# Attention by pairs of heads on the two halves of the TensorE array: unpadded keys, probabilities normalized before the transposes, values as the stationary operand, output laid out by features

## The chip, the cores and the metric

One core of one Trainium2 chip. The metric is device time in microseconds of one execution of the whole program (two layers of a small diffusion model), median of the runs; a change under about 3.4 us (0.2%) can hardly be told from none.

## The reference, cut to what matters

Each of two layers mixes tokens with a windowed softmax attention beside an mLSTM, and then applies an FFN (layer 0) or a mixture of 8 experts (layer 1). Attention has 8 query heads on 2 key heads of 64 features. It is computed three times: for 256 context tokens against themselves (layer 0; K = 256 keys), and for 256 image tokens against their window and the context (layers 0 and 1; K = 512 keys). All of it is float32.

```python
def sink_attention(qg, kv_sets, sink_g):            # per head: one extra logit, the sink, without a value
    s = einsum('bqhgd,bkhd->bhgqk', qg, k); s = where(mask, s, -inf); m = max(sink, s.max(-1))
    p = exp(s - m); denom = exp(sink - m) + p.sum(-1)
    return einsum('bhgqk,bkhd->bhgqd', p, v) / denom
def merge_groups(att, h_ml, o_pre, g_att, g_ml, w_out):
    att_n = rmsnorm(att, g_att)                      # over the 512 features of a token
    ml = headwise_rmsnorm(h_ml) * g_ml * sigmoid(o_pre)
    return concatenate([att_n, ml], -1) @ w_out
```

## The kernel before

Activations are kept feature-major (`xT`, and their split into a high and a low float32r part, `aH` and `aL`). A weight block comes by one DMA of 1 MB into a `raw` tile, ACT and DVE split it into H and L (L123, L124), and a product is three float32r matmuls (`mm3`, recorded at L227). Plain float32 matmuls, as in attention, appear in the trace as two MATMUL rows each.

`Mix.attention` (L926 to L1012) walks over 16 items, (query block of 128 tokens, head). `score` multiplies the 128 queries of two heads by the head's keys; `KV` holds each key head twice, in the upper and in the lower 64 partitions, with zeros in the other half, so that a head's matmul contracts over 128 partitions of which 64 are zero. `top` (DVE) adds the mask, takes the maximum over the keys and clips it by the sink; `expo` (ACT) makes the probabilities `P` and their sum; `trans` (PE) transposes P by blocks of 128 keys; `evac` copies the transposes to `pT`, in turn by DVE and ACT; `pv` makes pT the stationary operand (128 columns) and streams the 64 columns of the values `VA`. After 8 heads `pvout` (L988 to L997) computes the denominators, divides, and sums squares. `attention_out` (L1020 to L1042) scales the token-major AO by the root mean square, transposes it in 8 blocks and splits it into `aH` and `aL`.

The generator yields between its steps; `weave` interleaves it in program order with its neighbours: layer 0's context attention with the projections, the image attention of both layers with the mLSTM (`ml`) and with filler matmuls (layer 0: modulation products on 32-column tiles of the array, `ps_f<-raw,csil`, and the output projection; layer 1: the projection of the output gates, `ps_f<-aH,H`). The engines then work through an order that a scheduler sets from that program when the kernel is built; each engine keeps it strictly. PSUM banks are shared: two for scores (`s`), two (`t`) for the transposes, the mLSTM's value products and its transposes, one for the attention output (`o`).

The lines that the change and the steps of the prediction touch: KV L691, L705, L831, L841; score, top, expo, trans, evac, pv, pvout L940 to L997; attention_out L1026 to L1041; the mLSTM's end in layer 1: its normalization L1167, its transposes and products L1174, aH L1177 and aL on POOL L1178; the attention part of aL L1040.

## Time and profile before

| | |
|---|---|
| time, median of 3 runs (lowest to highest) | 1695.44 us (1695.27 to 1697.46) |
| profiled execution: span from first to last instruction | 1694.2 us, 1.2 us below the median (a time of its own is not listed for it) |
| mean granted TensorE clock | 0.991 |
| busy, of the span | PE 98%, PEld 82%, DVE 79%, ACT 60%, POOL 6% |
| matmul rows | 9194 |

How to read it: a MATMUL row's duration is its latency, and rows overlap; what a matmul costs is the distance from its start to the next start. Busy time alone therefore says little; the timeline, the windows and the chain of waits say which engine sets the pace of a stretch. The context attention runs from 101 to 155 us, the image attention of layer 0 from 180 to 241 us, and that of layer 1 from 769 to 830 us.

### The profile page before, as it was taken

To read this page: it belongs to the slowest core of one execution; us is meant where nothing else is said; L and a number is where in the kernel's file an instruction comes from. 1 tells how busy PE (TensorE), PEld (TensorE's weight loads), DVE (VectorE), ACT (ScalarE), POOL (GpSimd) and SP (SyncE) were. 2 spreads that over 40 slices of the span, in tenths; PEclk is the share of its full clock that TensorE was granted. 3 is DMA by queue.
4 is the path that set the end of the run, shared out by engine and by line. 5 is a ranking of instruction groups with operands and counts; after the bars stand their busy time and mean duration, and the time that the engine had idled before them with its cause. 6 is when DMAs were issued, how large, how long until landed. Compare 5 with 4: busy or idle time off the path is not lost.

```text
span 1694.2 us, 24338 instructions
## 1 busy us (share of the span) xinstructions
PE 1653.5 (98%) x9194; PEld 1392.9 (82%) x9194; DVE 1344.4 (79%) x2100; ACT 1008.1 (60%) x1466; POOL 105.7 (6%) x152
## 2 busy tenths in 40 slices
PE   8999999999999999999999999999999999999996
PEld 6779789988888889897898888888888888888885
DVE  3484678887667735788768898999999899998987
ACT  5533555642223224635548777877787777877775
POOL 2310111100000000201110000000000000000001
PEclk8999999999999999999999999999999999999998
DMA  9322544565548814441086999999999999999990
GB/s 309 116 66 75 169 155 140 160 223 182 170 166 278 297 63 138 142 139 51 26 326 230 359 356 353 336 354 364 352 353 321 368 361 357 341 333 358 357 340 27
DMA packets 222637, 407.08 MB, mean 240 GB/s; under 512 B 9776, under 2 KB 106288, under 8 KB 222512
## 3 DMA queue, kind: packets, MB, share of 16 engines
q1 hardware_dynamic: 220464, 404.38, 68.9%
q8 instruction: 74, 1.21, 0.3%
q10 hardware_dynamic: 2048, 1.07, 0.2%
q14 instruction: 51, 0.42, 0.1%
HBM read 404.38 MB, written 1.05 MB: 239 GB/s over the span
## 4 chain that ended last, share of the span: by engine, by line
PE 88%; DVE 7%; issue 2%; ACT 2%; DMA 1%; POOL 1%; ACTq 0%; DVEq 0%; POOLq 0%
PE ps_mm L227 57%; PE ps_s L227 17%; PE ps_t L227 4%; PE ps_t L231 3%; PE ps_f L227 3%; PE ps_o L227 2%; DVE L L124 2%; PE ps_sb L227 1%; DVE ca L776 1%; ACT H L123 1%; DMA tok<-in_x 0%; PE ps_mb L227 0%; DVE xn L539 0%; DMA raw<-in_w_mod 0%; POOL aL L551 0%
## 5 line engine op out<-in xcount | busy, mean ns | idle before, releaser
L123 ACT ACTIVATE H<-raw 128x1024 fp32r<-128x1024 f32 (+1 forms) x676 | 702.6, 1050 | 394.4 <-PE ps_mm L227 295.0
L124 DVE TENSOR_TENSOR L<-raw,H 128x1024 fp32r<-128x1024 f32 (+1 forms) x671 | 802.8, 1221 | 140.0 <-ACT H L123 134.4
L227 PE MATMUL ps_mm<-H,X 128*128 128x512 f32 (+1 forms) x1536 | 461.2, 379 | 0.0
L227 PEld LDWEIGHTS ps_mm<-H,X 128*128 128x128 f32 x1536 | 280.8, 188 | 55.9
L227 PE MATMUL ps_mm<-L,X 128*128 128x512 f32 (+1 forms) x768 | 288.6, 376 | 0.0
L227 PE MATMUL ps_mm<-aL,H 128*128 128x512 f32 (+1 forms) x752 | 257.8, 343 | 5.0 <-POOL aL L551 2.3
L227 PE MATMUL ps_mm<-aH,H 128*128 128x512 f32 (+1 forms) x752 | 259.5, 347 | 2.4 <-ACT aH L542 2.3
L227 PE MATMUL ps_mm<-aH,L 128*128 128x512 f32 (+1 forms) x752 | 256.4, 342 | 0.0
L227 PEld LDWEIGHTS ps_mm<-L,X 128*128 128x128 f32 x768 | 144.9, 189 | 27.5
L227 PEld LDWEIGHTS ps_mm<-aL,H 128*128 128x128 f32 x752 | 143.1, 190 | 22.8 <-POOL aL L551 3.1
L227 PEld LDWEIGHTS ps_mm<-aH,H 128*128 128x128 f32 x752 | 142.6, 191 | 21.6 <-ACT aH L542 2.5
L227 PEld LDWEIGHTS ps_mm<-aH,L 128*128 128x128 f32 x752 | 142.7, 190 | 16.6 <-DVE L L124 0.4
L227 PE MATMUL ps_s<-H,hH 128*128 128x512 f32 x352 | 140.5, 399 | 0.0
L227 PE MATMUL ps_s<-L,hH 128*128 128x512 f32 x352 | 139.1, 395 | 0.0
L227 PE MATMUL ps_s<-H,hL 128*128 128x512 f32 x352 | 138.8, 394 | 0.0
L611 DVE SCALAR_TENSOR_TENSOR macc<-raw,csil,macc 128x1024 f32<-128x1024 f32 x70 | 87.6, 1282 | 4.2 <-DMA raw<-in_w_mod 3.7
L227 PEld LDWEIGHTS ps_s<-H,hL 128*128 128x128 f32 x352 | 66.1, 188 | 15.9
L227 PEld LDWEIGHTS ps_s<-H,hH 128*128 128x128 f32 x352 | 66.2, 188 | 14.1
L227 PEld LDWEIGHTS ps_s<-L,hH 128*128 128x128 f32 x352 | 66.2, 188 | 13.8
L227 PE MATMUL ps_mm<-fH,H 128*128 128x512 f32 (+1 forms) x224 | 77.3, 346 | 0.0
L227 PE MATMUL ps_mm<-fL,H 128*128 128x512 f32 (+1 forms) x224 | 77.2, 345 | 0.0
L227 PE MATMUL ps_mm<-fH,L 128*128 128x512 f32 (+1 forms) x224 | 77.0, 344 | 0.0
(351 smaller groups left out, 2132.8 us busy)
## 6 DMA issues: line engine op xcount, KB each, us to landing
raw<-in_exp_w SPq DMA_DIRECT2D x264, 1024.0 KB, 5.9
raw<-in_w_mod SPq DMA_DIRECT2D x48, 1024.0 KB, 5.4
raw<-in_ffn_w SPq DMA_DIRECT2D x34, 1024.0 KB, 5.4
raw<-in_w_in SPq DMA_DIRECT2D x18, 1024.0 KB, 5.7
raw<-in_w_out SPq DMA_DIRECT2D x12, 1024.0 KB, 5.3
raw<-in_ffn_w SPq DMA_DIRECT2D x8, 768.0 KB, 4.5
tok<-in_ctx SPq DMA_DIRECT2D x2, 512.0 KB, 4.7
tok<-in_x SPq DMA_DIRECT2D x2, 512.0 KB, 7.0
```

What stands on the lines that cost most here:

```text
L123: nc.scalar.activation(h, src, AF.Copy)
L124: eng.tensor_tensor(l, src, h.bitcast(F32), op=OP.subtract)
L227: return self.eng.matmul(o, a, b, **kw)
L231: return self.eng.transpose(o, a, i)
L611: V.scalar_tensor_tensor(a, raw[:, q], c, a, op0=OP.mult, op1=OP.add)
L776: V.scalar_tensor_tensor(a, u[:, j:j + T], vc[:, w + 4 * j + chunk:w + 4 * j + chunk + 1], a, op0=OP.mult, op1=OP.add)
```

## The change

Items are now (query block, pair of heads): 8 per call instead of 16.

- KV loses its zero halves: key head kv stands in both halves of the partitions. The two scores of a pair contract over 64 partitions each, one on the upper and one on the lower 64 rows of the array, into two PSUM banks.
- The sink's exponential is taken per head (ACT, 128x1), the denominator is formed at once (`norm`), and ACT scales P in SBUF by its reciprocal before the transposes.
- The product with the values has VA as the stationary operand (64 columns, one half of the array's columns for each head) and streams the 128 columns of pT. The output comes with features on the partitions: O[64 features of a head, tokens].
- pvout is one ACT copy. attention_out squares and sums over features by ACT and DVE, reduces over the partitions with matmuls (`rstd_rows`), and multiplies by gain and norm on DVE; the 8 transposes and the ACT scaling go. Half of the low parts aL goes to POOL.
- A step of the generator yields four times instead of twice; the pools of P and pT have 4 buffers instead of 3.

```diff
-            self.KV = m.tile([128, 2, 2, 2 * T], F32, name="KV")
+            self.KV = m.tile([128, 2, 2 * T], F32, name="KV")
...
-            G.memset(self.KV, 0.0)
...
-            items = [(qb, h) for qb in range(2) for h in range(8)]
+            items = [(qb, c) for qb in range(2) for c in range(4)]
...
             def score(i):
-                PE.matmul(Sc[i][:, :K], Q[:, h // 2, qb * 128:(qb + 1) * 128], KV[:, h // 4, h % 2, :K],
-                          start=True, stop=True)
+                Sc[i] = [bank("s"), bank("s")]
+                for hf, r in halves:
+                    PE.matmul(Sc[i][hf][:, :K], Q[r, c, qb * 128:(qb + 1) * 128], KV[r, c // 2, :K],
+                              start=True, stop=True)
...
+                for hf, _ in halves:
+                    h = 2 * c + hf
+                    act(st[:, 2, qb, h:h + 1], sinkb[:, l, h:h + 1], AF.Exp, bias=st[:, 0, qb, h:h + 1])
+
+            def norm(i):
+                a, b, d = (st[:, k, qb, 2 * c:2 * c + 2] for k in (1, 2, 3))
+                V.tensor_tensor(d, a, b, op=OP.add)
+                V.reciprocal(d, d)
+                for hf, _ in halves:
+                    e = P[i][hf]
+                    act(e[:, :K], e[:, :K], AF.Copy, scale=d[:, hf:hf + 1])
...
             def pv(i):
                 for kb in range(nk):
-                    PE.matmul(O[qb][:, h * 64:h * 64 + 64], pt[:, kb * 128:(kb + 1) * 128],
-                              VA[:, kb, h // 4 * 64:h // 4 * 64 + 64], start=kb == 0, stop=kb == nk - 1)
+                    for hf, r in halves:
+                        PE.matmul(O[qb][r, c * 128:(c + 1) * 128], VA[:, kb, c // 2 * 64:c // 2 * 64 + 64],
+                                  pt[hf][:, kb * 128:(kb + 1) * 128], start=kb == 0, stop=kb == nk - 1,
+                                  skip_group_check=True)
...
+                act(AO[:, :, qb * 128:(qb + 1) * 128], O.pop(qb).rearrange("p (c q) -> p c q", c=4), AF.Copy)
...
-            for t in range(n + 5):
+            for t in range(n + 4):
                 at(expo, t - 1)
                 at(score, t)
-                at(trans, t - 3)
-                at(pv, t - 4)
+                at(pv, t - 3)
                 yield
-                at(evac, t - 3)
-                at(pvout, t - 4)
+                at(norm, t - 1)
                 at(top, t)
+                at(pvout, t - 3)
+                yield
+                at(trans, t - 1)
+                yield
+                at(evac, t - 1)
                 yield
...
         def attention_out(self, s):
-            for qb in range(2):
-                act(AO[:, qb], AO[:, qb], AF.Copy, scale=r[:, qb:qb + 1])
+            for j in range(4):
+                if j == 0:
+                    act(acc, AO[:, j], AF.Square)
+                else:
+                    q = tmp("sqa")
+                    act(q, AO[:, j], AF.Square)
+                    V.tensor_tensor(acc, acc, q, op=OP.add)
+            r = rstd_rows(acc, 512)
...
+            for j in range(4):
+                f = tmp("af")
+                V.scalar_tensor_tensor(f, AO[:, j], col("g_att", l * 4 + j), r, op0=OP.mult, op1=OP.mult)
+                H = aH[:, j, SL[s]]
+                act(H, f, AF.Copy)
+                (V, G)[j % 2].tensor_tensor(aL[:, j, SL[s]], f, H.bitcast(F32), op=OP.subtract)
```

How the order moves, at three places. The first is PE in the image attention of layer 1, in its second half, before (ps_s: scores; kc,P: transposes of probabilities; VA and pT: product with the values; VM and PTm: the mLSTM's product; ps_f: filler):

```order
L227 MATMUL ps_s<-KV,Q_x 128x512
L231 MATMUL ps_t<-kc,P 128x128 x4
L227 MATMUL ps_o<-VA,pT 128x64 x4
L227 MATMUL ps_t<-VM_c,PTm 128x129 x2
L227 MATMUL ps_t<-VM_x,PTm 128x129 x2
L227 MATMUL ps_t<-VM_c,PTm 128x129 x2
L227 MATMUL ps_t<-VM_x,PTm 128x129
L227 MATMUL ps_s<-KV,Q_x 128x512
L231 MATMUL ps_t<-kc,P 128x128 x4
L227 MATMUL ps_o<-VA,pT 128x64 x4
```

and of the change:

```order
L227 MATMUL ps_s<-KV,Q_x 128x512 x2
L231 MATMUL ps_t<-kc,P 128x128 x4
L227 MATMUL ps_o<-pT,VA 64x128 x8
L227 MATMUL ps_f<-aH,H_7379 128x256
L227 MATMUL ps_f<-aL_91,H_7379 128x256
L227 MATMUL ps_f<-aH,L_7380 128x256
L231 MATMUL ps_t<-kc,P 128x128 x4
L227 MATMUL ps_f<-aH,H_7419 128x256
L227 MATMUL ps_f<-aL_89,H_7419 128x256
```

A head's score, transposes and product became a pair's, and work on the whole array stands between two blocks on halves of it.

The second place is PE in the image attention of layer 0, near its middle, in the change (csil: modulation products on quarters of the columns):

```order
L227 MATMUL ps_o<-pT,VA 64x128 x8
L227 MATMUL ps_f<-raw_2071,csil 32x256
L227 MATMUL ps_t<-VM_c,PTm 128x129 x3
L227 MATMUL ps_s<-KV,Q_x 128x512
L231 MATMUL ps_t<-kc,P 128x128 x4
L227 MATMUL ps_s<-KV,Q_x 128x512
L227 MATMUL ps_f<-raw_2071,csil 32x256 x2
L227 MATMUL ps_t<-VM_c,PTm 128x129 x3
L227 MATMUL ps_f<-raw_2071,csil 32x256 x5
L231 MATMUL ps_t<-kc,P 128x128 x4
```

Before, a csil block stood whole (x8) and a score alone; now the two halves of this pair stand apart, with transposes between them, and the 8 csil matmuls of a block stand in three pieces (1, 2 and 5).

The third place is DVE at the end of layer 1's mixing (HM: the mLSTM's output, scaled by its norm; aL_89, aL_90 and af: attention's part of the output projection's operand; mf: the mLSTM's part), before:

```order
L124 TENSOR_TENSOR L_8146<-raw_7213,H_8145 128x1024
L513 SCALAR_TENSOR_TENSOR nb<-nb,nv 128x8
L1040 SCALAR_TENSOR_TENSOR aL_89<-ps_t,vc,aH 128x256
L515 SCALAR_TENSOR_TENSOR ny<-nb,nc 128x8
L1167 TENSOR_SCALAR HM<-HM,ny 128x128
L1040 SCALAR_TENSOR_TENSOR aL_90<-ps_t,vc,aH 128x256
L1040 SCALAR_TENSOR_TENSOR aL_89<-ps_t,vc,aH 128x256
L1167 TENSOR_SCALAR HM<-HM,ny 128x128
L1040 SCALAR_TENSOR_TENSOR aL_90<-ps_t,vc,aH 128x256
L1167 TENSOR_SCALAR HM<-HM,ny 128x128 x6
L1174 SCALAR_TENSOR_TENSOR mf<-ps_t,vc,SG_x 128x256 x3
```

and of the change:

```order
L515 SCALAR_TENSOR_TENSOR ny<-nb,nc 128x2
L515 SCALAR_TENSOR_TENSOR ny<-nb,nc 128x8
L1185 TENSOR_SCALAR HM<-HM,ny 128x128 x3
L1055 SCALAR_TENSOR_TENSOR af<-AO,vc,ps_t 128x256 x4
L1058 TENSOR_TENSOR aL_89<-af,aH 128x256
L1185 TENSOR_SCALAR HM<-HM,ny 128x128
L1058 TENSOR_TENSOR aL_90<-af,aH 128x256
L1185 TENSOR_SCALAR HM<-HM,ny 128x128 x4
L1192 SCALAR_TENSOR_TENSOR mf<-ps_t,vc,SG_x 128x256 x2
```

Four af products and two differences stand between the pieces of HM where four differences stood, and the two norms' root steps, of 128x2 and 128x8, now run side by side just ahead of it.

## Rows read from the trace of the kernel before

**Rows 1.** The page: busy time of each engine (share of the span, instructions), and the chain that ended last, by engine.

```profile
PE 1653.5 (98%) x9194; PEld 1392.9 (82%) x9194; DVE 1344.4 (79%) x2100; ACT 1008.1 (60%) x1466; POOL 105.7 (6%) x152
PE 88%; DVE 7%; issue 2%; ACT 2%; DMA 1%; POOL 1%; ACTq 0%; DVEq 0%; POOLq 0%
```

**Rows 2.** Busy time by windows: length, then busy us (instructions) of PE, PEld, DVE, ACT, POOL, granted clock, DMA share, GB/s. The first three hold the three attention calls; then the FFN, and the experts.

```profile
100.00:179.00 79.00, 77.95 (x490) 68.86 (x493) 44.98 (x120) 30.57 (x85) 8.34 (x16) 0.98 0.17 54
179.00:300.00 121.00, 118.95 (x965) 100.40 (x957) 100.46 (x341) 66.99 (x172) 17.00 (x40) 1.00 0.51 166
768.00:846.00 78.00, 76.32 (x523) 64.56 (x521) 61.55 (x201) 42.69 (x114) 14.31 (x26) 0.98 0.13 41
300.00:700.00 400.00, 396.81 (x2173) 340.44 (x2172) 276.24 (x390) 139.10 (x204) 16.71 (x20) 1.00 0.57 186
900.00:1600.00 700.00, 699.86 (x3316) 575.82 (x3315) 642.55 (x655) 552.46 (x619) 0.00 (x0) 1.00 0.98 348
```

**Rows 3.** Timeline of PE in the image attention of layer 0: start, us from the first start to the last end, then the operation, rows x count, array rows*columns in use, moving operand.

```profile
180.96 0.28 PE L227 MATMUL ps_mb<-MRH_c,one 128*128 128x256 f32 x1
181.07 0.28 PE L227 MATMUL ps_mb<-MRL_c,one 128*128 128x256 f32 x1
181.28 1.07 PE L227 MATMUL ps_f<-raw,csil 128*32 128x256 f32 x16
182.28 1.13 PE L227 MATMUL ps_s<-KV,Q_x 128*128 128x512 f32 x2
183.24 0.83 PE L227 MATMUL ps_t<-VM_c,PTm 128*128 128x129 f32 x6
183.91 1.03 PE L227 MATMUL ps_sb<-QM_c,KM_c 128*128 128x256 f32 x4
...
190.02 0.60 PE L231 MATMUL ps_t<-kc,P 128*128 128x128 f32 x4
190.46 1.03 PE L227 MATMUL ps_sb<-QM_c,KM_c 128*128 128x256 f32 x4
191.33 1.02 PE L227 MATMUL ps_s<-KV,Q_x 128*128 128x512 f32 x2
192.18 0.83 PE L227 MATMUL ps_t<-VM_c,PTm 128*128 128x129 f32 x6
192.85 0.60 PE L231 MATMUL ps_t<-kc,P 128*128 128x128 f32 x4
193.29 1.00 PE L227 MATMUL ps_o<-VA,pT 128*128 128x64 f32 x8
194.13 0.39 PE L231 MATMUL ps_f<-kc,modrow 128*128 128x128 f32 x2
```

**Rows 4.** The same view in the context attention of layer 0: matmuls that use 36 rows of the array, and one head's score.

```profile
148.91 0.56 PE L227 MATMUL ps_o<-VA,pT 128*128 128x64 f32 x4
149.40 0.25 PE L231 MATMUL ps_f<-kc,Fc 36*128 36x36 f32 x1
149.49 0.23 PE L231 MATMUL ps_f<-kc,g 36*128 36x36 f32 x1
149.55 0.23 PE L231 MATMUL ps_f<-kc,Fc 36*128 36x36 f32 x1
149.70 0.50 PE L227 MATMUL ps_mm<-aH,H 128*128 128x512 f32 x1
...
155.06 0.59 PE L227 MATMUL ps_s<-KV,Q_c 128*128 128x256 f32 x2
155.49 0.38 PE L231 MATMUL ps_t<-kc,P 128*128 128x128 f32 x2
```

**Rows 5.** The same view behind layer 0's mixing: a sum over partitions as `rstd_rows` makes it, and the float32r matmul behind it.

```profile
290.97 0.61 PE L227 MATMUL ps_f<-ones,sqacc 128*128 128x1 f32 x4 [0.47 <-DVE sqacc L491]
291.44 0.36 PE L227 MATMUL ps_mm<-aH,H 128*128 128x256 f32 x1
291.64 0.28 PE L227 MATMUL ps_mm<-aL,H 128*128 128x256 f32 x1
291.76 0.28 PE L227 MATMUL ps_mm<-aH,L 128*128 128x256 f32 x1
```

**Rows 6.** By tile, the vector work of attention: count, then the shortest, median and longest in ns, first and last start, forms.

```profile
L950 DVE TENSOR_TENSOR ps_s<-ps_s,kc x32: 280/299/300, 181.6 to 817.6; 128x128 f32<-128x128 f32 x32
L952 DVE TENSOR_REDUCE ast<-ps_s x48: 412/680/692, 103.0 to 817.9; 128x1 f32<-128x512 f32 x32, 128x1 f32<-128x256 f32 x16
L953 DVE TENSOR_TENSOR ast<-ast,nsink x48: 140/152/516, 103.4 to 819.1; 128x1 f32<-128x1 f32 x48
L958 ACT ACTIVATE P<-ps_s,ast x48: 456/680/722, 104.0 to 820.1; 128x512 f32<-128x512 f32 x32, 128x256 f32<-128x256 f32 x16
L958 ACT ACTIVATION_READ_ACCUMULATOR P<-ps_s,ast x48: 188/193/243, 104.4 to 820.7; 128x1 f32 x48
L989 ACT ACTIVATE ast<-ast x6: 195/208/248, 132.7 to 822.0; 128x8 f32<-128x8 f32 x6
L991 DVE RECIPROCAL ast<-ast x6: 191/194/203, 134.3 to 822.9; 128x8 f32<-128x8 f32 x6
L1026 ACT ACTIVATE AO<-AO,ny x6: 707/710/725, 171.9 to 834.3; 128x512 f32<-128x512 f32 x6
```

**Rows 7.** Timelines at the end of layer 1's mixing (engine in the third column): the mLSTM's norm and its operand on DVE, POOL's low part, and the two idle times of PE in the output projection (in brackets, with what ended them).

```profile
836.15 0.17 DVE L520 TENSOR_SCALAR nv<-ss 128x8 f32<-128x8 f32 x1 [0.47 <-ACT junk L1136]
839.08 0.47 DVE L1040 SCALAR_TENSOR_TENSOR aL<-ps_t,vc,aH 128x256 fp32r<-128x256 f32 x1
842.67 0.87 DVE L1174 SCALAR_TENSOR_TENSOR mf<-ps_t,vc,SG_x 128x256 f32<-128x256 f32 x2
843.67 3.79 POOL L1178 TENSOR_TENSOR aL<-mf,aH 128x256 fp32r<-128x256 f32 x4 [1.00 <-ACT aH L1177]
...
844.46 0.39 PE L227 MATMUL ps_mm<-aL,H 128*128 128x256 f32 x1 [0.25 <-POOL aL L1178]
846.12 0.39 PE L227 MATMUL ps_mm<-aL,H 128*128 128x256 f32 x1 [1.04 <-POOL aL L1178]
```

More of the change, by code (lines that the diff above doesn't have):

```diff
@@ L930, in attention @@
             wm, KV, VA, Q = self.wm, self.KV, self.VA, self.Q[s]
[L931 removed]
+            AO = wm.tile([128, 4, T], F32, tag="AO", name="AO", bufs=1)
             st = wm.tile([128, 4, 2, 8], F32, tag="ast", name="ast", bufs=2)
[L933 to L935 removed]
+            self.AO[s] = AO
+            items = [(qb, c) for qb in range(2) for c in range(4)]
@@ L936, in attention @@
             n = len(items)
             Sc, P, TB, PT, O = {}, {}, {}, {}, {}
+            halves = [(hf, slice(hf * 64, hf * 64 + 64)) for hf in range(2)]
             def score(i):
-                qb, h = items[i]
-                Sc[i] = bank("s")
-                PE.matmul(Sc[i][:, :K], Q[:, h // 2, qb * 128:(qb + 1) * 128], KV[:, h // 4, h % 2, :K],
-                          start=True, stop=True)
-            def top(i):
-                qb, h = items[i]
-                p = Sc[i]
-                if s == "x":
-                    kb, m = ((3, m01), (2, m10))[qb]
-                    V.tensor_tensor(p[:, kb * 128:(kb + 1) * 128], p[:, kb * 128:(kb + 1) * 128], m, op=OP.add)
-                m = st[:, 0, qb, h:h + 1]
-                V.tensor_reduce(m, p[:, :K], axis=AX.X, op=OP.max, negate=True)
-                V.tensor_tensor(m, m, nsink[:, l, h:h + 1], op=OP.min)
@@ L955, in expo @@
-            def expo(i):
-                qb, h = items[i]
-                e = P[i] = wm.tile([128, 512], F32, tag="P", name="P", bufs=3)
-                act(e[:, :K], Sc.pop(i)[:, :K], AF.Exp, bias=st[:, 0, qb, h:h + 1],
-                    accum_out=st[:, 1, qb, h:h + 1])
-            def trans(i):
-                t = TB[i] = bank("t")
-                e = P.pop(i)
-                for kb in range(nk):
-                    PE.transpose(t[:, kb * 128:(kb + 1) * 128], e[:, kb * 128:(kb + 1) * 128], ident)
@@ new lines, in top @@
+            def top(i):
+                qb, c = items[i]
+                for hf, _ in halves:
+                    p = Sc[i][hf]
+                    if s == "x":
+                        kb, m = ((3, m01), (2, m10))[qb]
+                        V.tensor_tensor(p[:, kb * 128:(kb + 1) * 128], p[:, kb * 128:(kb + 1) * 128], m, op=OP.add)
+                    h = 2 * c + hf
+                    V.tensor_reduce(st[:, 0, qb, h:h + 1], p[:, :K], axis=AX.X, op=OP.max, negate=True)
+                m = st[:, 0, qb, 2 * c:2 * c + 2]
+                V.tensor_tensor(m, m, nsink[:, l, 2 * c:2 * c + 2], op=OP.min)
@@ new lines, in expo @@
+            def expo(i):
+                qb, c = items[i]
+                P[i] = []
+                for hf, _ in halves:
+                    h = 2 * c + hf
+                    e = wm.tile([128, 512], F32, tag="P", name="P", bufs=4)
+                    P[i].append(e)
+                    act(e[:, :K], Sc[i][hf][:, :K], AF.Exp, bias=st[:, 0, qb, h:h + 1],
+                        accum_out=st[:, 1, qb, h:h + 1])
+                Sc.pop(i)
+                for hf, _ in halves:
+                    h = 2 * c + hf
+                    act(st[:, 2, qb, h:h + 1], sinkb[:, l, h:h + 1], AF.Exp, bias=st[:, 0, qb, h:h + 1])
@@ new lines, in norm @@
+            def norm(i):
+                qb, c = items[i]
+                a, b, d = (st[:, k, qb, 2 * c:2 * c + 2] for k in (1, 2, 3))
+                V.tensor_tensor(d, a, b, op=OP.add)
+                V.reciprocal(d, d)
+                for hf, _ in halves:
+                    e = P[i][hf]
+                    act(e[:, :K], e[:, :K], AF.Copy, scale=d[:, hf:hf + 1])
+            def trans(i):
+                TB[i] = []
+                for e in P.pop(i):
+                    t = bank("t")
+                    TB[i].append(t)
+                    for kb in range(nk):
+                        PE.transpose(t[:, kb * 128:(kb + 1) * 128], e[:, kb * 128:(kb + 1) * 128], ident)
@@ L975, in pv @@
+            def evac(i):
+                PT[i] = []
+                for hf, src in enumerate(TB.pop(i)):
+                    pt = wm.tile([128, 512], F32, tag="pT", name="pT", bufs=4)
+                    PT[i].append(pt)
+                    if hf:
+                        act(pt[:, :K], src[:, :K], AF.Copy)
+                    else:
+                        V.tensor_copy(pt[:, :K], src[:, :K])
             def pv(i):
-                qb, h = items[i]
+                qb, c = items[i]
                 pt = PT.pop(i)
-                if h == 0:
+                if c == 0:
@@ L984, in pvout @@
             def pvout(i):
-                qb, h = items[i]
-                if h < 7:
+                qb, c = items[i]
+                if c < 3:
                     return
-                V.tensor_tensor(st[:, 2, qb], st[:, 0, qb], sinkb[:, l], op=OP.add)
-                act(st[:, 2, qb], st[:, 2, qb], AF.Exp)
-                V.tensor_tensor(st[:, 3, qb], st[:, 1, qb], st[:, 2, qb], op=OP.add)
-                V.reciprocal(st[:, 3, qb], st[:, 3, qb])
-                V.tensor_tensor(AO[:, qb].rearrange("p (h d) -> p h d", h=8),
-                                O.pop(qb).rearrange("p (h d) -> p h d", h=8),
-                                st[:, 3, qb].rearrange("p (h a) -> p h a", a=1).to_broadcast([128, 8, 64]),
-                                op=OP.mult)
```

40 lines of the change are left out of this document (9 added, 31 removed).

## The prediction

> **What bounds the kernel now.** I read the page first, then the windows of the three attention calls, then PE's timeline in them, then the vector engines' rows, last the end of layer 1's mixing. PE is busy for 98% of the span and makes 88% of the chain that ended last [rows 1]. In the windows that hold attention it is busy for 77.95 of 79, 118.95 of 121 and 76.32 of 78 us; ACT stands at 39%, 55% and 55% there, DVE at 57%, 83% and 79%. In the FFN and the experts PE is busy throughout [rows 2]; the change leaves the order there as it is, so a microsecond that PE wins or loses in attention moves the end by one. DMA is at 0.13 to 0.51 in attention. So the change is priced in PE starts, and then it is asked where PE would have to wait.
>
> **What PE's rows cost.** The distance of starts counts. A head's score is two rows: 191.33 to 192.18, 0.86 us (K = 512); 0.43 us for K = 256 [rows 3, 4]. Its product with the values is 8 rows from 193.29 to 194.13, 0.84 us, or 0.21 per matmul of two rows [rows 3]; these stream only 64 columns each, so loading 128 weight columns is what they cost. Four transposes take 0.44 us (190.02 to 190.46), as they will afterwards.
>
> **Part 1: halves side by side.** That tiles of the array work at once is seen here for quarters of the columns: 16 csil rows of 256 columns take 1.00 us [rows 3], while 16 such rows one by one would take 3.4 us (0.215 each, by the two of the 256-key score [rows 4]). Halves of the columns with different moving data are the same case; halves of the rows are not shown by any row. I take both as fully side by side when the two stand together. The new order has 24 pairs of scores; 19 stand together, 5 are parted (3 in layer 0's image call, 1 in each other). Saved: 12 image pairs x 0.86 + 7 context pairs x 0.43 = 13.3 us. The value product keeps 160 matmuls, 0.21 each, 33.6 us in all; they now stream 128 columns. The nearest rows, 6 mLSTM products of 129 columns in 0.67 us [rows 3], make a matmul of two 0.224. In the new order they need 88 slots of one or two (80 would do if none were parted): 19.7 us. Saved: 13.9. Together 27.2 us.
>
> The Trainium skill weighs against full overlap: "TensorE: Matmul & The Clock Gate", Part 3, gives measured speedups of 3.07 for four row tiles and 2.38 for three column tiles. By these (0.77 and 0.79 of the ideal), as an estimate, the paired scores and products would take 8 us more than in my sum. The csil rows reach 3.4 of 4 with the cost of leaving included, 3.8 without, so the sum goes by the rows.
>
> **Part 2: changing the tiling.** Going to and from a part of the array costs PE time. Into csil: 181.07 to 181.28, 0.21 against the 0.11 of the step before. Out of it: 1.00 instead of 4 x 0.215 = 0.86, and the score behind it takes 0.96 instead of 0.86, since nothing hides its weight load [rows 3]. The 36-row matmuls show the same for rows: 0.49 instead of 0.42 going in, 0.15 instead of 0.06 coming out [rows 4]. So an entry costs 0.10 for emptying the array, and up to 0.10 more for an unhidden load of 128 columns. I take 0.20 for an entry into the row halves (128 columns), 0.15 for the column halves (64), 0.18 back to the whole array, 0.12 into csil. Counted in the new order beyond those of the old: 29 into row halves, 35 into column halves, 51 back, 7 more into csil: 5.8 + 5.2 + 9.2 + 0.8 = 21.1 us. Bounds: 0.10 each makes 12 us, 0.20 each 24. The higher end is nearer, because a score behind csil shows both parts each time.
>
> **Part 3: what the new order cuts up.** In layer 0's image call the csil blocks of 8 matmuls no longer stand whole; pieces of 1 to 8 need 30 groups of up to four where 24 did. 6 x 0.43 (a group is two rows deep, 0.215 each) = 2.6 us.
>
> **Part 4: attention_out.** 24 transposes go: 24 x 0.11 = 2.6 us. Three calls of rstd_rows come: 4 rows of one column, 0.47 us [rows 5], and 4 rows of 128 columns, 4 x 0.11 [rows 3], so 2.8 us. Net +0.2. The KV memset lies on POOL, busy 8.34 of 79 us [rows 2]; at no cost, and its cover stays.
>
> PE's own sum: -27.2 + 21.1 + 2.6 + 0.2 = **-3.3 us**. By call: context -0.7, layer 0 image +1.7, layer 1 image -4.4, and 0.2 for part 4.
>
> **Part 5: what PE may have to wait for.** ACT gets, per image call, 16 scalings of 512 columns in SBUF (nearest row L1026, 0.71) and 16 sink exponentials (L989, 0.21), 14.7 us, and loses about 2 us (two L1026, two L989, partly replaced by squares) [rows 6]. In layer 1 that takes ACT from 42.69 to some 55 of 78 us [rows 2], 71%; no bound by itself. DVE gains 8 sums and reciprocals (0.35 together) and loses 8 of the 16 minima (0.15) [rows 6]: +1.6 us. The chain from a pair's scores to its first transpose: two masks and maxima (2 x 0.98), a minimum 0.15, two exponentials with their sums read out (2 x 0.8), two sinks 0.42, a scaling 0.71: 4.8 us, plus what stands between on DVE and ACT. The scaling waits on ACT for DVE's reciprocal, and behind it queue the mLSTM's exponentials and the copies of pT. By the new order, at the prices above, PE has 5.7 to 7.5 us of other work between these two points in layer 1, and over 8 in layer 0. I allow 1.5 us of waits, all in layer 1 (nothing to 8).
>
> The end of layer 1's mixing is a chain off PE: the mLSTM's last product, its norm on DVE from 836.15, mf from 842.67, POOL's low parts to 847.46, and PE idles 0.25 and 1.04 us for them [rows 7]. Two things change there. Of the filler, 42 matmuls stood behind the mLSTM's last product and 33 do now, so 9 x 0.12 = 1.1 us moves ahead of it while the chain behind stays. And DVE has, between the norm and mf, six attention operations where it had four (0.47 each), three sums of squares ahead, and the two root chains side by side: about 2.0 us more. So 3.1 us of layer 1's 4.4 are given back there.
>
> **Sum.** -3.3 + 1.5 + 3.1 = +1.3 us on the profiled span of 1694.2; the median of the runs stands 1.2 above that span, so **1696.8 us**, which is no change that can be told (0.2%, 3.4 us).
>
> **Rivals.**
> - *Cheaper switches.* If the emptying alone counts (0.10), because PE often waits at those points anyway or the loads hide, part 2 is 12 us: 9 us better, 1687.8; with no waits in part 5's middle, 1686. For it: the first transposes behind a block load data that is ready. Against: every csil row shows the exposed load.
> - *The row halves overlap poorly.* PE takes the two float32 rows of one score before it starts the other half, or the halves share a path. No row shows row tiles at work together. With no overlap 13.3 us are lost: 1710; with the partial overlap of the skill's figures above, about 1705. This ends slower; it decides when a pair of scores of 512 keys takes over 1.1 us from its first start to the next block.
> - *The vector engines set layer 1's pace.* If the scaling waits behind mLSTM work on ACT in most of the 16 image pairs, at 0.5 us each beyond my 1.5: some 6 us more, 1703. For it: 83% and 79% on DVE and a chain through three strictly ordered engines. Against: the order gives 5.7 us or more of cover. The Trainium skill speaks for it: "TensorEngine Tiling (Array Packing)", PSUM Bottleneck, says that tiling speeds TensorE and not the emptying of PSUM, which then may bound.
>
> **How the numbers follow.** My forecast 0.44, cheaper switches 0.25, poor row overlap 0.13, vector engines 0.18. The forecast's own range is 1692 to 1701, most of it within 0.2%. Faster by over 0.2%: the second case and a little of the first, 0.27. Slower: the last two and the upper end of the first, 0.34. The same: 0.39. The range reaches from the cheap switches to the row halves without overlap, 1686 to 1709.
>
> **What would show it.** Right: a score pair's four rows in about 0.86 us, starting in twos a few ns apart; eight value products in some 0.9 us; 0.10 us more at each change of tiling and a longer first row behind it; PE idle at the end of layer 1 grown to 3 us or more while its chain through DVE and POOL stands. Wrong: scores that start one after another (second rival), first rows behind a block that are not longer (first), or idle PE before the transposes of P in layer 1 that add up to over 4 us (third). If PE's idle time in the three windows falls and the switches cost as said, my end of layer 1 is wrong.

## The result, and the profile after

The changed kernel takes **1709.1 us** (median of 6 runs, 1706.5 to 1710.4) beside 1696.4 us for the kernel before on the same chip: a ratio of 1.0067, 95% interval 1.0049 to 1.0085. It is slower, by over three times what can be told from no change; the forecast was no change, 1696.8. The profiled execution took 1708.6 us (span 1706.9, granted clock 0.986; before 1694.2 and 0.991). PE is busy 5 us longer in a span that is 12.7 us longer; ACT gained 31 us [rows 1]:

```profile
PE 1658.6 (97%) x9194; PEld 1373.5 (80%) x9194; DVE 1344.7 (79%) x2115; ACT 1039.0 (61%) x1556; POOL 107.6 (6%) x156
PE 86%; DVE 7%; ACT 2%; issue 2%; POOL 1%; DMA 1%; ACTq 0%; POOLq 0%; DVEq 0%
```

The windows that answer to [rows 2], in the same columns. In the third, layer 1's attention, PE is idle for 7.9 of 78 us where it was 1.7; but 3.4 of these are a wait ahead of layer 1 (for Fc, 3.42 us in both kernels) that ended just ahead of this window before, at 767.83, and lies inside it now. The clock of the first and third fell from 0.98 to 0.96; FFN and experts stand as before.

```profile
100.00:179.00 79.00, 77.31 (x472) 61.79 (x473) 41.71 (x107) 38.08 (x113) 7.49 (x12) 0.96 0.17 54
179.00:300.00 121.00, 118.60 (x947) 89.11 (x946) 98.97 (x351) 76.34 (x200) 21.87 (x46) 1.00 0.48 157
768.00:846.00 78.00, 70.10 (x489) 52.24 (x488) 57.39 (x174) 52.55 (x139) 11.70 (x25) 0.96 0.09 29
300.00:700.00 400.00, 396.51 (x2168) 339.99 (x2168) 276.94 (x375) 142.47 (x210) 15.43 (x18) 1.00 0.57 184
900.00:1600.00 700.00, 699.86 (x3317) 575.64 (x3317) 639.87 (x658) 553.19 (x623) 0.00 (x0) 1.00 0.96 343
```

Cut at the same PE rows, the two profiles differ by stretch as follows (us; the forecast's parts beside):

| stretch | before | after | difference | forecast |
|---|---|---|---|---|
| start, to the qt product behind PE's long wait | 99.6 | 100.4 | +0.8 | 0 |
| context call, to the first csil row | 78.8 | 80.0 | +1.2 | -0.7 |
| layer 0's image call and FFN, to layer 1's Fc transposes | 590.8 | 594.1 | +3.3 | +1.7 |
| layer 1, to the mLSTM's last product | 64.9 | 66.3 | +1.4 | -4.4 + 1.5 + 1.1 |
| from there to the router's first product | 17.3 | 22.9 | +5.6 | 3.1 - 1.1 |
| the rest, to PE's last row | 829.0 | 829.4 | +0.4 | 0 |

Of the 5.6 us, 1.9 are 16 small router products (wr,mods) that stood behind that mark before; nine filler products (1.1 us) moved the other way, ahead of the mLSTM's last product.

The same 12.7 us by kind of time, over the whole span to PE's last row. Both profiles hold the same 9194 matmul rows. PE is at work at half clock for 19.2 us before and 34.3 after; what that costs is an estimate, its lower value from rows of one form (Pt products of 128x256: 0.21 us from start to start at half clock, 0.12 at full), its upper one from rows that take twice as long. PE's rows are what is left.

| | before | after | difference | forecast |
|---|---|---|---|---|
| idle time of PE | 27.2 | 34.8 | +7.6 | 1.5 + 3.1 |
| cost of half clock (estimate) | 8.4 to 9.6 | 15.0 to 17.2 | +6.6 to +7.6 | 0 |
| PE's rows at full clock (estimate) | | | -1.5 to -2.5 | -3.3 |

So the rows gained nearly what was forecast. The loss is idle time and the clock.

**The halves.** PE in layer 0's image call (start, us, rows):

```profile
189.57 0.64 PE L227 MATMUL ps_f<-raw,csil 128*32 128x256 f32 x8
190.14 1.13 PE L227 MATMUL ps_s<-KV,Q_x 64*128 64x512 f32 x4
191.20 0.38 PE L227 MATMUL ps_mb<-MRH_c,one 128*128 128x256 f32 x1
...
195.02 1.12 PE L227 MATMUL ps_s<-KV,Q_x 64*128 64x512 f32 x2
196.07 0.71 PE L227 MATMUL ps_t<-VM_c,PTm 128*128 128x129 f32 x4
...
199.99 0.88 PE L227 MATMUL ps_o<-pT,VA 128*64 128x128 f32 x12
200.79 0.66 PE L231 MATMUL ps_t<-kc,P 128*128 128x128 f32 x4
```

A pair of scores takes 1.06 us (190.14 to 191.20), and one half alone takes 1.05 (195.02 to 196.07). So two halves run wholly side by side. The 0.20 us over the forecast's 0.86 are the changes of tiling on both sides, which the forecast counts apart in part 2, and not the price of a row on half the array: with scores on the whole array (run 3 below), four rows take 1.71 us between other rows on the whole array and 1.92 between two blocks on parts of it, the same 0.20 more.

```profile
224.66 1.88 PE L227 MATMUL ps_s<-KV,Q_x 128*128 128x512 f32 x4
226.37 0.60 PE L231 MATMUL ps_t<-kc,HM 128*128 128x128 f32 x4
...
232.44 1.99 PE L227 MATMUL ps_s<-KV,Q_x 128*128 128x512 f32 x4
234.36 0.88 PE L227 MATMUL ps_o<-pT,VA 128*64 128x128 f32 x12
```

Six value matmuls (12 rows) take 0.80 us with a change of tiling on both sides, 0.13 each, where one took 0.21.

**The end of layer 1.** PE, then ACT behind the mLSTM's last product (in brackets, idle time and what ended it):

```profile
841.81 0.28 PE L227 MATMUL ps_f<-aH,L 128*128 128x256 f32 x1
844.89 0.39 PE L227 MATMUL ps_f<-aH,H 128*128 128x256 f32 x1 [2.80 <-ACT SG_x L918]
845.11 0.28 PE L227 MATMUL ps_f<-aL,H 128*128 128x256 f32 x1
845.23 0.28 PE L227 MATMUL ps_f<-aH,L 128*128 128x256 f32 x1
...
848.33 0.41 PE L227 MATMUL ps_f<-aH,L 128*128 128x256 f32 x1
848.54 0.41 PE L227 MATMUL ps_f<-aH,H 128*128 128x256 f32 x1
...
851.98 2.02 PE L227 MATMUL ps_f<-wr,mods 128*128 128x8 f32 x16 [1.08 <-ACT SG_x L918]
```

```profile
842.01 1.06 ACT L123 ACTIVATE H<-raw 128x1024 fp32r<-128x1024 f32 x1 [2.63 <-PE ps_f L227]
842.97 0.29 ACT L1154 ACTIVATE junk<-HM 128x128 f32<-128x128 f32 x1
...
843.26 1.01 ACT L1048 ACTIVATE sqa<-AO 128x256 f32<-128x256 f32 x3
844.18 0.29 ACT L1154 ACTIVATE junk<-HM 128x128 f32<-128x128 f32 x1
...
844.47 0.36 ACT L918 ACTIVATE SG_x<-ps_f 128x256 f32<-128x256 f32 x1
```

PE's next om projection needs bank f, which SG_x empties on ACT. ACT takes its work in order: ahead of SG_x stand a weight split that waited for PE, and then the new squares of the attention output (sqa). Before the change the same wait was 0.43 us, since the squares were not there and eight transposes of AO gave PE work:

```profile
836.31 1.03 PE L231 MATMUL ps_t<-kc,AO 128*128 128x128 f32 x8
837.77 0.39 PE L227 MATMUL ps_f<-aH,H 128*128 128x256 f32 x1 [0.43 <-ACT SG_x L920]
```

The second thing to see is the distance of PE's starts: 0.12 us at 845, 0.21 at 848. The granted clock fell to half behind the idle time, for 3.4 us from 846.9 and again from 853.7. By windows (the granted clock stands behind the five engines' busy times), first after, then the same place before:

```profile
840.00:844.00 4.00, 2.09 (x16) 1.70 (x15) 3.06 (x12) 1.99 (x6) 0.00 (x0) 1.00 0.00 0
844.00:848.00 4.00, 3.11 (x20) 2.94 (x21) 3.03 (x21) 0.84 (x4) 0.53 (x1) 0.86 0.67 198
848.00:852.00 4.00, 2.92 (x17) 2.68 (x16) 2.81 (x14) 1.40 (x3) 0.00 (x0) 0.71 0.19 64
852.00:856.00 4.00, 4.00 (x26) 4.00 (x27) 3.77 (x11) 1.57 (x5) 1.81 (x3) 0.72 0.00 0
856.00:860.00 4.00, 4.00 (x31) 4.00 (x31) 2.18 (x4) 1.79 (x4) 3.51 (x4) 0.86 0.00 0
```

```profile
844.00:848.00 4.00, 2.71 (x19) 2.14 (x19) 2.42 (x4) 1.90 (x3) 3.46 (x4) 1.00 0.18 33
852.00:856.00 4.00, 4.00 (x38) 4.00 (x38) 3.24 (x5) 1.38 (x3) 0.00 (x0) 1.00 1.04 378
```

**Two older places.** Ahead of layer 0's qt products PE idled 3.00 us before and 5.31 after: a scheduler put a weight split on ACT (H) behind a convolution step, in a part that the change does not touch. First before, then after, the wait and the windows:

```profile
99.57 1.22 PE L227 MATMUL ps_t<-qt,kc 128*128 128x256 f32 x2 [3.00 <-ACT qt L866]
...
100.00:103.00 3.00, 3.00 (x9) 2.37 (x9) 1.90 (x6) 0.00 (x0) 2.84 (x4) 0.59 0.01 3
103.00:106.00 3.00, 3.00 (x15) 2.48 (x14) 1.14 (x4) 0.74 (x3) 1.18 (x3) 1.00 0.00 0
```

```profile
100.35 1.22 PE L227 MATMUL ps_t<-qt,kc 128*128 128x256 f32 x2 [5.31 <-ACT qt L864]
...
100.00:103.00 3.00, 2.65 (x7) 1.72 (x9) 1.90 (x3) 0.30 (x2) 2.84 (x4) 0.50 0.01 3
103.00:106.00 3.00, 3.00 (x9) 1.96 (x10) 1.56 (x6) 1.33 (x7) 1.56 (x3) 0.50 0.00 0
```

The stretch at half clock is 3.4 us long before and 6.8 after. It goes with the idle time: in the twelve profiles that have this wait it is 3.4 us behind 2.5 to 3.0 us of idle time (six profiles), and 6.8 us or more behind 4.6 to 5.3 us (six). At layer 1's start the same idle time of 3.42 us stands in both kernels, yet the half clock behind it lasts 3.4 us before and 6.8 after, where PE waited 0.49 us more for qt in between.

### The profile page after: what moved, and what is told of

The parts are those of the page before. It is cut to its first block, busy times and chain, and to the rows that moved or that the text cites. A ratio compares the mean times of both kernels' runs of the same rounds, so it can differ in the third digit from the quotient of the medians.

```text
span 1706.9 us, 24450 instructions
## 1 busy us (share of the span) xinstructions
PE 1658.6 (97%) x9194; PEld 1373.5 (80%) x9194; DVE 1344.7 (79%) x2115; ACT 1039.0 (61%) x1556; POOL 107.6 (6%) x156
## 3 DMA queue, kind: packets, MB, share of 16 engines
HBM read 404.38 MB, written 1.05 MB: 238 GB/s over the span
## 4 chain that ended last, share of the span: by engine, by line
PE 86%; DVE 7%; ACT 2%; issue 2%; POOL 1%; DMA 1%; ACTq 0%; POOLq 0%; DVEq 0%
PE ps_mm L227 56%; PE ps_s L227 16%; PE ps_t L227 5%; PE ps_f L227 3%; PE ps_t L231 3%; DVE L L124 2%; PE ps_o L227 2%; PE ps_sb L227 1%; ACT H L123 1%; DVE ca L775 1%; POOL aL L551 0%; DMA tok<-in_x 0%; DVE xn L539 0%; PE ps_mb L227 0%; PE ps_mm L1462 0%
```

## The experiments

Three theories went in. **A**: the loss is the clock, half speed behind longer idle times of PE. **B**: it is PE's rows, halves that gain less and changes of tiling. **C**: the end of layer 1 is set by a chain on the vector engines, whatever PE does. All runs are compared with the kernel before.

One reading came only with the runs. Each run has its time and its mean granted clock; the 73 runs of the kernel before that list their clock go from 1694.5 us at a clock of 0.993 to 1704.8 at 0.986. With span x (1 - clock) as the clock lost in a run, the runs of one kernel lie near a line: over the 175 runs of all 14 kernels 0.67 us per us lost, and the spread within a kernel falls from 1.6 to 0.65 us. With this slope, an estimate, the mean of each kernel splits into its clock and the rest (us over the mean of the kernel before, 1697.8; the rest is good to about 0.6). The split takes for granted that lost clock costs between two kernels what it costs between the runs of one; no run shows that, and the few runs of the single kernels alone give slopes from 0.4 to 1.0. It also cannot say whether an edit caused the clock that it removes.

| run | kernel | median | ratio (95%) | clock | rest |
|---|---|---|---|---|---|
| | the change | 1709.1 | 1.0067 (1.0049 to 1.0085) | 6.1 | 5.1 |
| 1 | change, idle places filled | 1713.6 | 1.0087 (1.0074 to 1.0100) | -0.7 | 15.6 |
| 2 | before, idle places filled | 1704.0 | 1.0034 (1.0022 to 1.0046) | -0.7 | 7.0 |
| 3 | whole-array scores, layer 0 | 1706.1 | 1.0053 (1.0040 to 1.0066) | 3.8 | 5.0 |
| 4 | whole-array values, layer 0 | 1708.8 | 1.0063 (1.0050 to 1.0076) | 4.7 | 5.6 |
| 5 | own bank for an om projection | 1705.5 | 1.0047 (1.0033 to 1.0060) | 4.2 | 3.6 |
| 6 | squares on POOL | 1702.9 | 1.0033 (1.0022 to 1.0044) | 1.0 | 4.1 |
| 7 | 5 and 6 | 1705.1 | 1.0042 (1.0028 to 1.0056) | 4.0 | 2.9 |
| 8 | before, ACT delayed | 1697.6 | 1.0001 (0.9992 to 1.0009) | -0.4 | 0.1 |
| 9 | early sums of squares | 1706.8 | 1.0042 (1.0028 to 1.0056) | 4.1 | 4.3 |
| 10 | 3 and 4 | 1704.3 | 1.0038 (1.0027 to 1.0048) | 3.2 | 3.4 |
| 11 | 9 and 3 | 1702.6 | 1.0028 (1.0018 to 1.0039) | 2.7 | 2.3 |
| 12 | 10 and 6 | 1701.4 | 1.0019 (1.0010 to 1.0028) | 1.2 | 2.2 |

**1 and 2: PE kept busy where it idles.** A helper `hold`, called at the places named, and `warm(17)` in the experts' start:

```diff
+        def hold(self, tag, rhs, n):
+            w = bank(tag)
+            for _ in range(n):
+                nc.tensor.matmul(w[:, :128], ident, rhs, start=True, stop=True)
```

> The changed kernel, with products of no use put on PE at four places where it is idle: 20 of 128 columns at 96 us (before the qt products of layer 0), 15 at 770 us (before the Fc transposes of layer 1), 13 behind the mLSTM's last product of layer 1 (842 us), 17 of 256 columns at 893 us (before the second Pt product of the experts). The output stays the same. Theory A, the clock: at each of these places the trace shows the granted clock at half for 6.8 us or so in all (3.4 us lost each, 13.7 us together; before the change three such places lost 1.7 us each, 5.2 together), so most of the 12 us is lost there. If the clock stays at 1.00, the four places give back up to 13.7 us: 1695 to 1701 us. Theory B, the rows: the 12 us are PE's own rows (pairs of scores at 1.05 us instead of 0.86, changes of the tiling) and waits, and the clock only makes the waits look longer: 1706 us or more.

> The kernel before the change, with the same products of no use at its three idle places (12 at 97 us, 15 at 764 us, 17 at 881 us); its layer 1 ends without a stretch at half clock. Theory A: the three places lose 1.7 us each, so 1691 to 1693 us. What then separates this run from the changed kernel with the same filling is what the change costs in rows and waits: some 4 to 6 us. Theory B: within 2 us of the kernel before, 1694 to 1697 us, and the two kernels stay about 12 us apart.

Both times are misses, and the filling is why. At the first place its operand came at the end of the wait and not at its start; at the second the scheduler laid qt products between it, and it ran behind their waits. Both times it stood in the way:

```profile
97.28 6.70 PE L717 MATMUL ps_o<-KM_c,kc 128*128 128x128 f32 x40 [5.60 <-DVE KM_c L794]
...
778.51 0.70 PE L227 MATMUL ps_t<-qt,kc 128*128 128x256 f32 x2 [1.65 <-ACT qt L874]
779.05 1.28 PE L717 MATMUL ps_o<-g,kc 128*128 128x128 f32 x10
```

The totals say nothing for or against A. Two places of run 1 went as meant. At the experts' start the fill is a clean test, because the wait for Pt stays as long as it was (2.6 us from the first Pt product to the second in both). First the change, then run 1:

```profile
895.59 1.15 PE L227 MATMUL ps_mm<-Pt,tt 128*128 128x256 f32 x3 [2.20 <-DVE Pt L1543]
...
902.08 0.39 PE L227 MATMUL ps_mm<-H,X 128*128 128x512 f32 x1
```

```profile
900.62 2.20 PE L1475 MATMUL ps_mm<-cR 128*128 128x256 f32 x17
903.04 0.96 PE L227 MATMUL ps_mm<-Pt,tt 128*128 128x256 f32 x3 [0.22 <-DVE Pt L1556]
...
907.19 0.39 PE L227 MATMUL ps_mm<-H,X 128*128 128x512 f32 x1
```

The 31 Pt rows take 6.5 us in the change, at half clock (0.50 from 896 to 900), and 4.2 in run 1 at 1.00: 2.3 us went with products of no use in the idle time. The other place is layer 1's end, where the 13 products (26 rows) fill the wait for SG_x; behind them the clock stays at 1.00:

```profile
849.46 3.06 PE L717 MATMUL ps_mb<-PTm,kc 128*128 128x128 f32 x26
...
856.00:860.00 4.00, 2.92 (x25) 2.68 (x24) 3.80 (x8) 2.89 (x6) 1.91 (x2) 1.00 0.08 16
```

From the mLSTM's last product to the router's first it takes 20.0 us instead of 22.9. These stretches do not hold the same rows: in run 1 the 16 router products (1.9 us) stand behind it, as in the kernel before, and nine filler products more (1.1) stand in it. For the same rows it is some 2 us less, although the fill took 3.1 us. That is A at both places: useless work in an idle time makes the stretch behind it faster. Runs 1 and 2 also compare layer 1 ahead of it (Fc transposes to last mLSTM product) nearly undisturbed, with the same 54 om rows in it: 63.4 us for the kernel before, 62.7 with the change, of which some 0.5 is a rest of half clock at its start.

**3, 4 and 10: layer 0 on the whole array.**

```diff
-                    PE.matmul(Sc[i][hf][:, :K], Q[r, c, qb * 128:(qb + 1) * 128], KV[r, c // 2, :K],
+                    if l == 0:
+                        r = slice(0, 128)
+                    PE.matmul(Sc[i][hf][:, :K], Q[r, c, qb * 128:(qb + 1) * 128], KV[r, c // 2, hf * (1 - l), :K],
...
+                        if l == 0:
+                            W.now += 128 / 2400.0
+                            nc.tensor.matmul(O[qb][:, c * 128:(c + 1) * 128],
+                                             VA[:, kb, c // 2, 64 - hf * 64:192 - hf * 64],
+                                             pt[hf][:, kb * 128:(kb + 1) * 128], start=kb == 0 and hf == 0,
...
```

> The changed kernel with the scores of layer 0 (8 context pairs, 8 image pairs) on the whole array with zero-padded keys, as before; layer 1 keeps row halves. Prices from the trace after: a pair in halves takes 1.05 us for 512 keys and 0.63 for 256, on the whole array 1.72 and 0.86, so 8 x 0.67 + 8 x 0.23 = 7.2 us come back. If a change of the tiling costs what the prediction took (0.20 into the halves, 0.18 back, some 20 times in layer 0), 7.6 us go: no change, 1708 to 1710. If only the emptying counts (0.10 each way), 4 us go: 1712. If the row halves bring no gain at all, 1701 to 1703. Under theory A all three shift by up to 3.4 us with the idle places of PE, so the sum over layer 0's attention is read from its rows and landmarks.

> The changed kernel with the value products of layer 0 on the whole array: stationary values padded with zeros to 128 columns, both heads added up in one tile; layer 1 keeps column halves. The virtual time that paces the filler is kept as it was. A pair of 4 blocks takes 8 x 0.21 = 1.7 us instead of some 0.85, one of 2 blocks 0.85 instead of 0.43: 8 x 0.85 + 8 x 0.42 = 10.2 us come. At the prediction's prices some 24 entries of 0.15 and 24 returns of 0.18 go, 7.9 us: 1711 us. If the changes of tiling cost 0.10 each, 4.8 us go: 1714. If the vector engines and not PE set the pace in layer 0, no change: 1709.

> The changed kernel with scores and value products of layer 0 on the whole array (padded keys and padded values); early normalization, pairs of heads and the feature-major output stay, layer 1 keeps both halves. The stretch from the first csil product of layer 0 to the statistics behind its output projection took 112.6 us before the change and 117.2 after; with whole scores 116.9, with whole values 118.1. If the two parts add up, 117.9 us: then the halves together are worth 0.7 us there, and the 4.6 us come from what is left of the change (normalization, order). If the halves with their changes of tiling cost 1.7 us, as the prediction has it, 115.5 us. If they cost all, 112.6. The whole run: 1706 to 1710 us.

Whole scores: 1706.1, none of the cases expected (the 7.2 and the 7.6 us of that text overlap, since its 1.05 us already holds a change into the halves and one out); what the run gained on the change is clock. Ahead of qt PE idled 2.99 us again and the context stretch took 78.8 us instead of 80.0; the rest is 5.0 against 5.1. Layer 0's stretch is 116.9 against 117.2: nothing gained, nothing lost. Whole values: rest 5.6, no change that can be told, where the prediction's prices wanted 2.3 us more and the cheap changes of tiling 5. Both: 1704.3, under the 1706 to 1710 expected, and 115.9 us in the stretch. That mark deceives, since some 17 rows of the output projection stand ahead of it in the change and not in this run; with the FFN behind it, to layer 1's Fc transposes, it is 592.5 against 594.1 after and 590.8 before.

These stretches mix rows and waits, and the waits hide what the rows do. Split as in the second table, the rows of layer 0's attention and FFN take about 0.8 us more than in the change with whole scores, 2.9 with whole values and 2.5 with both (estimates), while PE idles 1.3, 2.2 and 3.1 us less. So the halves with their changes of tiling do save PE some 2.5 us of rows in layer 0, and longer waits take them back; why the waits are longer was not tested. B explains none of the loss in layer 0.

**5 to 7: the wait for SG_x.**

```diff
-                p = bank(tag)
+                p = bank("mb" if l and key == "om1" and sub == 0 else tag)
...
-                    act(q, AO[:, j], AF.Square)
+                    if l:
+                        G.tensor_tensor(q, AO[:, j], AO[:, j], op=OP.mult)
+                    else:
+                        act(q, AO[:, j], AF.Square)
```

> The changed kernel; the third om projection of layer 1 gets the PSUM bank of the mLSTM's row values instead of bank f, so its first product no longer waits for the ACT operation SG_x that empties f (2.80 us idle at 844.9 us). Theory A (the wait for SG_x and the half clock behind it are what the end of layer 1 lost): idle falls to 1 us or less (the weights' high part is then last), the clock stays at 1.00, 3 to 4 us go: 1705 to 1706 us. Theory C (the end of layer 1 is set by the chain sums of squares, root, af, low parts on DVE, whatever PE does meanwhile): PE only waits later, at the output projection, and at most 1 us goes: 1708 to 1709.

> The changed kernel; three of the four squares of the attention output in layer 1 are made by POOL instead of ACT. ACT loses 1.0 us ahead of SG_x, and the sums of squares no longer stand behind the split of weights on ACT (842.0 to 843.1 us). Theory A: the wait for SG_x falls from 2.8 to some 1.8 us, and if the clock then stays at 1.00 another 1.7 us or more goes: 1705.5 to 1708. Theory C: the sums are ready some 2 us sooner, and the output projection starts as much sooner: 1706 to 1707, with PE's wait for SG_x still there.

> The changed kernel with both: own bank for the third om projection and three squares on POOL. Theory A: the two gains of the wait are one, so no better than the own bank alone, 1704.5 to 1706. Theory C: the chain sets the pace, so like the squares on POOL alone or 1 us better, 1705 to 1707; if wait and chain are both there, the gains add up and the output projection of layer 1 starts 5 us sooner than in the changed kernel: 1703 to 1704.

With its own bank PE no longer waits there, but later, for the root on DVE:

```profile
845.37 1.95 PE L227 MATMUL ps_f<-wr,mods 128*128 128x8 f32 x16 [0.47 <-ACT SG_x L918]
849.13 1.09 PE L227 MATMUL ps_t<-kc,ny 128*128 128x128 f32 x4 [1.81 <-DVE nb L511]
851.24 0.79 PE L227 MATMUL ps_mm<-aH,H 128*128 128x256 f32 x2 [0.81 <-ACT aH L1057]
```

The stretch is 21.6 us, 1.3 less: that is C, a wait that moves on. The time is what A expected, but not in A's way: the half clock is still there (6.8 us from 849.2). With the squares on POOL the sums come sooner, and the stretch takes 20.8 us: PE waits 3.2 us in it instead of 3.9, and the half clock lasts 3.4 us instead of twice 3.4:

```profile
840.62 0.39 PE L227 MATMUL ps_f<-aH,H 128*128 128x256 f32 x1 [1.59 <-ACT SG_x L918]
...
845.78 0.68 PE L227 MATMUL ps_t<-kc,ny 128*128 128x128 f32 x4 [1.14 <-DVE ny L515]
```

By its median this is the best single edit, 6.2 us and better than either theory had, but 5.0 of them are clock (0.989 against 0.985) and 1.0 is not; how much of that clock the shorter waits gave back, the split cannot say. Both together: rest 2.9, so 2.2 us, near the sum of 1.5 and 1.0; with 0.6 us on each of these, that both parts were there is likely and not shown. Its median is no better than the own bank's; its profile has the end of layer 1 at half clock for 10 us (845 to 855).

**8: the wait put into the kernel before.** Seven copies on ACT ahead of SG_x:

```diff
+                            if l and part == "om0" and sub == 1:
+                                for _ in range(7):
+                                    z = tmp("z")
+                                    act(z, p[:, SL[s]], AF.Copy)
                             act(self.SG[s][:, h], p[:, SL[s]], AF.Tanh, scale=0.5)
```

> The kernel before the change, with seven copies of 256 columns (0.36 us each, 2.5 us) on ACT ahead of the SG_x that the third om projection of layer 1 waits for: the wait that the change made, put into the kernel without it. Theory A: PE idles 2.9 us there instead of 0.43, the granted clock falls to half behind it, and the end comes 4 to 6 us later than before: 1701 to 1703. Theory C: the copies delay nothing on the chain that sets the output projection's start except what stands behind them on ACT: 2.5 us or less and no more, 1698 to 1700.

Inconclusive: the copies took 2.0 us, but the scheduler moved six om products from ahead of the mLSTM's last product to behind it, and PE waited 0.51 and 0.43 us for SG_x, not 2.9. The wait was not made, so nothing of A or C is told apart.

**9 and 11: sums of squares per block of queries.**

```diff
...
+                j = tmp("sqa", 512).rearrange("p (c q) -> p c q", c=4)
+                act(j, ao, AF.Square)
+                V.tensor_reduce(Q[:, qb, 0:128], j.rearrange("p c q -> p q c"), axis=AX.X, op=OP.add)
```

> The changed kernel with the squares of the attention output taken per block of queries, as soon as the block is copied from PSUM: one square of 512 columns on ACT and one sum over the four chunks on DVE, twice a call, instead of four squares and three sums at the end. Theory C (the chain from the last value product to the output projection sets the end of layer 1): behind the last copy one square and one sum (some 1.4 us) are left instead of 7 us in which a weight split stands; from the last mLSTM product to the router's first product it took 22.9 us (17.3 before the change, 20.8 with three squares on POOL), now 19.5 to 20.5, and the whole 1702 to 1705 us. Theory A (the wait of PE for SG_x): three squares of 0.33 us go from ahead of SG_x, the wait falls from 2.8 to 1.8 us, 1705 to 1708.

> The changed kernel with the early sums and with whole-array scores in layer 0: the two edits that cost nothing or gained. If they add up, each keeps what it showed: whole scores 0.2 us less in layer 0, the early sums as in their own run; 1701 to 1704 us, still 4 to 7 us above the kernel before. Under theory A, 1704 to 1707.

The end of layer 1 takes 19.9 and 19.7 us, as C expected (19.5 to 20.5), 3 us less than the change; the wait for SG_x, 0.43, is shorter than the 1.8 of A. The time of run 9 is a miss, 1706.8: layer 1 ahead of it grew to 68.2 us, and the clock lost 4.1. Run 11 came out as expected, 1702.6.

**12: both places together.**

> The changed kernel with scores and value products of layer 0 on the whole array and three squares of layer 1's attention output on POOL; from the change stay the pairs, the early normalization, the feature-major output, and both halves in layer 1. Alone the two edits gave 4.8 and 6.2 us of the 12 us. If they act in two places (layer 0 and its neighbourhood; the end of layer 1), they add up: 1698 us (1697 to 1700), within what can be told of the kernel before, and the two places hold nearly all of the loss. If the gains were largely the same thing (the clock at the places where PE idles ahead of layer 0's and layer 1's attention, which both runs had less of), they do not add up: 1702 us or more.

1701.4 lies between the two cases: the gains do not add up, 7.7 us of the 11.0. By rest they do (2.9 beside 1.7 + 1.0); it is the clock that both runs had less of. The best version stands 0.2% above the kernel before. No experiment pointed to one that beats it.

## Why the prediction was right or wrong

- **Part 1** held. Halves of the rows and of the columns stand wholly side by side, and the overlap rival is out (1.06 us, under its 1.1). The 0.86 us that were to show it hold no change of tiling, though the forecast itself puts one on each side of a pair. Two of the twelve image pairs that were counted as standing together start 0.43 and 0.58 us apart (at 234.39 and 796.47) and lose some 1.0 us of the gain. From start to start the scores fell by 5.2 us (28.3 to 23.5 and 6.6 to 6.2), the values by 7.9 (33.2 to 25.3), each with part of its changes of tiling, of waits and of half clock in it.
- **Parts 2 to 4** held. A row behind a change of tiling takes 0.10 us longer, one ahead of it 0.09, so an entry with 128 columns costs the 0.20 that was taken; the second case (nine us better) is out. The Trainium skill says of the cause ("TensorEngine Tiling (Array Packing)", Tiling Modes) that a change of the tiling mode drains the engine; the trace agrees, with some 0.1 us. The csil rows went from 20.3 to 24.6 us, of which 1.2 are waits behind them, so 3.2 beside the 3.4 forecast. Layer 0's stretch grew by 3.3 us, of which 1.6 are idle time and 1.7 PE's rows, as forecast. In layer 1 the change gains about 1.2 us of the stretch at full clock (runs 1 and 2) where 4.4 less 1.5 of waits were forecast: PE's rows gained 2.1 there and the waits cost 0.9.
- **Part 5, the middle,** was right: 1.13 us of waits for P and 0.49 for qt in layer 1, against 1.5. The third rival is out where it was put.
- **Part 5, the end of layer 1,** had the right place and nearly the right size, by the wrong chain: PE's waits there grew by 2.2 us (1.7 to 3.9), 3.1 less the filler's 1.1 were forecast. It counted DVE's sums and roots behind the last mLSTM product, and not that the squares stand on ACT ahead of SG_x, which frees the one bank of the filler. That the size agrees is luck. The other 3.4 us or so of this stretch are the half clock behind the waits.
- **The step that failed** is "a microsecond that PE wins or loses in attention moves the end by one". Every wait was counted at its own length, and the clock had no term at all. In the runs 6.1 of the 11.2 us between the means are clock; in the profiles half clock costs 6.6 to 7.6 us more than before. Run 1 shows this cost by itself at the experts' start, 2.3 us behind a wait of 2.2.
- **A second term put at nothing** is waits outside layer 1 ("all in layer 1"). PE idles 3.8 us more there: 0.9 up to layer 0's qt products, 0.3 in the context call, 1.6 in layer 0 and its FFN, 1.1 behind the router's first product. Their causes were not told apart by a run of their own.
- The time, 1709.1, lies at the very end of the range 1686 to 1709. That end was worked out for row halves without overlap, which did not happen, so that the range reaches so far is luck.
- In nine of the eleven profiles with the changed layer 1 a stretch at half clock follows the waits at its end; it is gone where that time was filled (run 1), and in run 11. The kernel before has none. A long wait is not the whole of it: in run 7 the half clock from 844.9 follows a wait of 0.47 us and a block of router products of 8 columns, and no wait over 0.5 us stands in the 70 us before.
- Open: what makes the half clock last 3.4 or 6.8 us behind the same idle time of 3.42 us (layer 1's start: 3.4 in eight profiles with that wait, 6.8 in four), and how much of the clock's 6.1 us is the change itself and how much how the scheduler happens to lay out the kernel; runs 3 and 6 show that small edits elsewhere move it by 2 to 5 us.

## What to carry to other kernels

Price a new wait of the tensor engine with the half clock that may follow it, and look at the granted clock behind the idle times of the kernel that is there. Split a change of time into the tensor engine's rows, its idle time and its time at half clock before a row's price is blamed, and price a row with its neighbours: the first behind a change of tiling and the last ahead of one cost more on any part of the array. When an operation is added to a strictly ordered engine, look for the small operation behind it that frees a single buffer. Between kernels that are 1% apart, compare at the same granted clock before a difference is put down to an edit.

## What the runs showed of the hardware

- Two row halves run wholly at once: a pair of float32 scores of 64x512 takes 1.06 us between two other tilings, one half alone 1.05. The row behind a change of tiling takes 0.53 us and the row ahead of one 0.52, on half the array and on the whole alike; a row of the whole array between its like takes 0.43. For 256 columns a pair takes 0.63 us, 0.20 more than two whole-array rows (0.43).
- The time of one and the same kernel moved by 10 us over 73 runs with the granted clock, 0.67 us for each us of clock lost.
- Idle PE for 2.80 us at the end of layer 1 was followed by half clock though PE had waited for no more than 0.5 us at a time in the 66 us before; 26 rows of no use in its place kept the clock at 1.00. At the experts' start 17 such rows in a wait of 2.2 us gave 2.3 us back.
